# A decoder trunk's embedding gate as seven block products in three passes, with sums of squares kept by accumulating transfers

## The chip, the cores and the metric

The kernel runs on one core of one Trainium2 chip. The metric is device time in microseconds (us), the median over runs. The engines are named as in the profile: PE is the matrix engine (PEld its weight loads), DVE the vector engine, ACT the scalar engine with its activation functions, POOL a general engine that here does elementwise adds and issues transfers, SP an engine that only issues transfers. A matmul multiplies a 128x128 weight block into up to 512 columns (tokens) and adds into a PSUM accumulator. Tiles live on chip with 128 partitions; names that end in `_d` are arrays in device memory (DRAM).

## The reference, cut to what matters

All tensors are float32; 1024 tokens, 2048 features, a per-token embedding `p` of 256.

```python
def rmsnorm(x, g, eps=NORM_EPS):
    y = xf * lax.rsqrt(jnp.mean(xf * xf, axis=-1, keepdims=True) + eps)
    return (y * g.astype(jnp.float32)).astype(x.dtype)
...
        hn = rmsnorm(h, norm_mix_g[i])
        proj = hn @ w_in[i]
...
        mixed = jnp.concatenate([sb_out * jax.nn.silu(sb_g), df_out * jax.nn.silu(df_g)], axis=-1)
        h = h + mixed @ w_out[i]

        gate = jax.nn.sigmoid(rmsnorm(h, norm_ple_g[i]) @ w_ple_gate[i])
        h = h + gate * (p[i] @ w_ple_proj[i])
    return rmsnorm(h, norm_final_g)
```

The change touches the last four of these lines: the out-projection (`w_out`), the gate (`w_ple_gate`, 2048x2048), the embedding's product (`w_ple_proj`, 256x2048) and the two norms around them. The attention before them is untouched.

## The kernel before, in words

Everything is transposed: a tile is 128 features by 512 tokens. The 1024 tokens are two halves of 512; half 1 goes first. 2048 features are 16 tiles, called by `ch` or `kt`.

**Precision.** Each float32 product is made of three matmuls in a faster 32-bit format. An operand x is split into a high part (`xh`, a copy by ACT that rounds) and a low part (`xl` = x - xh, a subtraction by DVE), and so is each weight; the three are xh*whi, xl*whi and xh*wlo. So each weight and each operand costs one ACT and one DVE operation ahead of its first matmul.

**Seven block products.** A product of two 2x2 block matrices takes eight block products; it can be done with seven if sums and differences of blocks are formed first. The class `Seven` (L574) does that for the v and gate projection (`gv`) and the out-projection (`op`, L1350): the operand blocks are half 1 and half 0 of the tokens by two groups of input features, the weight blocks the same groups by the output feature tiles u and u+8. The products are named by the operand they use: A11, A12 and A22 (plain blocks) and S1 to S4 (sums). Weight differences (`T1` to `T4`) are formed by DVE as each product's weights come due; `whigh` and `wlow` split them. `prod` does the twelve matmuls of a product and then splits one further weight and takes up to two entries off the queue `xq` of operand splits. The out-projection runs in two phases `ph`, each over half of the input features, because the operands of one phase fill the chip. In phase 0 the partial results are stored to `half_d`; in phase 1 they are read back (`hr`), added by DVE, and added onto `h_d` (which holds the residual) by an accumulating transfer that POOL issues (`put`, L1365).

**The gate, dense.** The gate comes after the last unit of the out-projection (L1538 on). Its operands are the 16 tiles of h for one half of tokens, times the norm's gain, split by `split` in `gate_loads` (half 1) or `split_scaled` (half 0). `unit(X)` (L218) makes one unit, the output tiles u and u+8 for one half: 4 pieces of 4 input tiles by 2 outputs by 3, 96 matmuls of 512 columns. Weights are loaded and split by `wprep` (L147), 1024 columns at a time, once for each half. First come the eight units of half 1, then the eight of half 0. The norm's root mean square is not needed ahead of the product, because it scales whole tokens: it is multiplied onto the result (`gated`, L1336).

**Around it.** `ple` makes the embedding's product (12 matmuls for each unit and half) into PSUM, and ACT copies it to the chip's memory. `gated` multiplies the gate's result by `rstd`, applies the sigmoid, multiplies by the embedding's product, adds to h, and adds the square of the new h to a sum. These sums of squares (`SumSq`, L101) are ACT squares and POOL adds; a matmul with a matrix of ones adds them over the partitions, and `rstd_from` makes the reciprocal root. `final` scales h and stores the output. The last unit of half 0 (u = 7) is done in two quarters of 256 tokens with weights that are all split ahead (`wz`), so that the first quarter's output is stored while the second is computed.

**Order.** TensorE's order is the order of the program. Up to the third unit of the gate, DVE and ACT also run in the order of the program (`man2`), and after that in an order that a scheduler picks. An engine works through its queue in order: an instruction that waits holds up all that stand behind it. The same holds for SP's and POOL's queues of transfers.

In the out-projection's phase 1 a unit goes A11, A22 of the unit before, S2, S4 of the unit before, A12, S1, S3. In the last unit, A12 (`p2`) stands after S3 instead, ahead of its own A22 and S4.

Of the kernel before, what the change touches and what calls it, by code (L numbers as in the profile page):

```python
# [52 lines left out]
def _body(ctx, nc, tc, ap):  # L53
# [113 lines left out]
    class Stream:  # L167
# [5 lines left out]

        def gates(self):
            units = [ap["w_gate"][u] for _ in range(2) for u in range(8)]
            self.todo = deque((w, pc) for w in units[:-1] for pc in range(4))
            return self.prep(later=True)
# [372 lines left out]
    with tc.tile_pool(name="at", bufs=2) as at, tc.tile_pool(name="pz", bufs=2, space=PSUM) as pz:  # L550
# [23 lines left out]
        class Seven:  # L574

            def __init__(self, w, n):
                self.w = w
                self.units = [(ph, u) for ph in range(2) for u in range(n)]
                self.wq, self.XC, self.T = {}, {}, {}
                self.made, self.late, self.slot = [], 0, 0  # L580
                self.xq = deque()
                self.after = None

            def places(self, nm, i):
                where, t = PLACE[nm][i]
# [7 lines left out]
            def split(self, nm, i, hi, lo, gain=None, raw=None):  # L593

                raw = lo.bitcast(F32) if raw is None else raw
                if gain is None:
                    A.copy(hi, raw)
                    V.tensor_tensor(lo, raw, hi.bitcast(F32), op=ALU.subtract)
                else:
                    A.activation(hi, raw, AF.Copy, scale=gain)  # L600
                    V.scalar_tensor_tensor(lo, raw, gain, hi.bitcast(F32), op0=ALU.mult, op1=ALU.subtract)
                self.XC[nm, i] = hi, lo
# [37 lines left out]
            def begin(self):  # L640
# [3 lines left out]
                self.todo = [e for n in range(len(self.units)) for e in self.sources(n)]  # L644

            def wload(self, n, *bs):
                if n < len(self.units):
# [13 lines left out]
            def sources(self, n):  # L661
# [14 lines left out]
                def t4():  # L676
# [5 lines left out]
                return [(n, nm, fn) for nm, fn in own + [("S2", t2), ("S1", lambda: self.T["T1"]), ("S3", t3),  # L682
                                                         ("S4", lambda: b22_), ("A22", t4)]]

            def whigh(self):
# [3 lines left out]
                n, nm, fn = self.todo[i]  # L689
# [6 lines left out]
                if nm == "S4":  # L696
                    A.activation(t[:, 0], src, AF.Copy, scale=-1.0)
                else:
                    A.copy(t[:, 0], src)  # L699
                self.made.append((src, t))  # L700

            def wlow(self):
# [4 lines left out]
                n, nm, _ = self.todo[i]  # L707
                src, t = self.made[i]
                self.made[i] = None
                if nm == "S4":  # L710
# [3 lines left out]
                ph, u = self.units[n]  # L714
                self.wq[u, ph, nm] = t[:, 0], t[:, 1]
                if nm == "S4":
                    self.wload(n + 2, 22)

            def lead(self):
                for _ in range(4):  # L720
# [4 lines left out]
            def prod(self, u, ph, nm, o, start):  # L725
                self.product(u, ph, nm, o, start)
                self.slot += 1
                self.whigh()
                self.wlow()
                self.after(u, ph, nm)  # L730
                for _ in range(2):
                    if self.xq and self.xq[0][0] <= self.slot:
                        self.xq.popleft()[1]()
# [22 lines left out]
        def split1(c, i):  # L756
            nm = ("A11", "A12")[c]
            gv.split(nm, i, *gv.places(nm, i), gain=gcol(KX[0][i][c]), raw=raw1[i][:, c, :])
# [9 lines left out]
        def combine(i):  # L768
# [4 lines left out]
            def one():  # L773
                gv.split("A22", i, *gv.places("A22", i), gain=gcol(kb), raw=b2)
# [9 lines left out]
        def divide(nm, i):  # L784
            raw = {"S1": raw2[i][1], "S3": raw2[i][0], "S2": raw1[i][:, 0, :], "S4": raw1[i][:, 1, :]}[nm]
            gv.split(nm, i, *gv.places(nm, i), gain=gcol(KX[0][i][0]) if nm == "S3" else None, raw=raw)
# [116 lines left out]
        def load_x(nm, i):  # L903

            hi, lo = gv.places(nm, i)
# [332 lines left out]
        h = {}  # L1238
        hpair = {}
        rst = {}  # L1240
        H1 = (None, None, "k2", "v2", "q", "k", "v", "cs")
        H0 = ("k2", "v2", "q", "bt", "bt", "bt", "pt", "pt")

        def pair(nm, tag, dt=F32, shape=(P, 2, HALF)):
            return at.tile(list(shape), dt, name=nm, tag=tag, bufs=BUFS.get(tag, 2))

        def rows2(nm, u):
            return ap[nm].rearrange("(a k p) t -> k p a t", a=2, p=P)[u]

        def gained(half, ch):  # L1250

            A.activation(h[half, ch], h[half, ch], AF.Copy, scale=gvec[:, 2, ch:ch + 1])

        def final(half, ts, r, us, eng=V):
            o = slice(half * HALF + ts.start, half * HALF + ts.stop)
            for u in us:
                hp = hpair.get((half, u))
                if half == 0 and u == 7:
                    for c in range(2):
                        t = h[half, u + 8 * c][:, ts]  # L1260
                        V.scalar_tensor_tensor(t, t, gvec[:, 2, u + 8 * c:u + 8 * c + 1], r, op0=ALU.mult, op1=ALU.mult)
                elif hp is not None:
                    t = hp[:, :, ts]
                    eng.tensor_tensor(t, t, r.unsqueeze(1).to_broadcast([P, 2, ts.stop - ts.start]), op=ALU.mult)
                else:
                    for c in range(2):
                        t = h[half, u + 8 * c][:, ts]
                        eng.tensor_tensor(t, t, r, op=ALU.mult)
                        nc.sync.dma_start(ap["out"][(u + 8 * c) * P:(u + 8 * c + 1) * P, o], t)
                if hp is not None:  # L1270
                    nc.sync.dma_start(rows2("out", u)[:, :, o], hp[:, :, ts])

        def load_h(half, u):
            tag = (H0, H1)[half][u]
            with tc.issue_after(lastw[0].ins):
# [452 lines left out]
```

## Time and profile before

| | us |
|---|---|
| median of 3 runs | 2491.54 |
| lowest, highest | 2489.08, 2492.83 |
| the profiled execution's own time | 2490.54 |
| its span in the profile | 2488.8 |
| out-projection's last stretch, up to the gate's first matmuls | 2040 to 2063 |
| gate, half 1 | 2063 to 2259 |
| gate, half 0, up to the last unit's quarters | 2273 to 2445 |

The span starts with the first instruction and ends with the last; the execution's own time adds what lies around it. Positions are us from the start of the span. A row of a group view reads: line, engine, operation, output and inputs, shape, count, then total busy time, mean ns of one, and the idle time of the engine just before them with what ended it. A row of single instructions reads: start, duration, engine, line, operation, output and inputs, and in brackets how long the engine stood idle before it and what released it. The granted clock is the share of full speed that the chip allowed TensorE.

### The profile page before, as it was taken

The page shows a single profiled execution, that of the slowest core. Times are in us where ns is not written, and L with a number is a line of the kernel's source. Part 1 is how long each engine was busy: PE and PEld are TensorE (multiplying, and loading weights), DVE is VectorE, ACT ScalarE, POOL GpSimd, SP SyncE. Part 2 cuts the span into 40 slices and gives each one's busy share as a digit, 9 for nine tenths or more (in the row PEclk, how much of TensorE's full clock was granted, in tenths as well). Part 3 has the DMA queues.
Part 4 walks back from the last instruction along what each step waited for, and adds up shares of the span by engine and source line. Part 5 has one row for each costly group of instructions (what it writes and reads, how often), then busy time and mean ns, then how long its engine had stood idle before and what let it go on. Part 6 is the DMA issues. An engine that isn't in the chain of part 4 may idle for free.

```text
span 2488.8 us, 31941 instructions
## 1 busy us (share of the span) xinstructions
PE 2413.1 (97%) x11434; PEld 2002.3 (80%) x11434; DVE 1810.9 (73%) x3010; ACT 1201.2 (48%) x2063; POOL 280.1 (11%) x361
## 2 busy tenths in 40 slices
PE   8999999999999999999999999998899999999997
PEld 6787878888888887888888888886787887787886
DVE  6788777778877778788888877877678674546555
ACT  5334335555555445565555555445423234546342
POOL 1211110000000000000000001110111113330110
PEclk9999999999999999999999999999999999999998
DMA  8776655444445556334444344555757777343433
GB/s 290 250 271 217 224 171 161 154 146 129 145 143 148 181 158 200 119 110 114 121 117 115 102 127 119 144 153 173 224 167 222 165 192 231 121 129 97 133 109 102
DMA packets 167471, 397.72 MB, mean 160 GB/s; under 512 B 18896, under 2 KB 23248, under 8 KB 167312
## 3 DMA queue, kind: packets, MB, share of 16 engines
q1 hardware_dynamic: 131040, 302.07, 37.7%
q0 software_dynamic: 36272, 93.60, 14.3%
q8 instruction: 90, 1.47, 0.2%
q14 instruction: 69, 0.57, 0.1%
HBM read 297.03 MB, written 106.95 MB: 162 GB/s over the span
## 4 chain that ended last, share of the span: by engine, by line
PE 82%; DVE 8%; DMA 4%; ACT 3%; issue 3%; SPq 0%; DVEq 0%; ACTq 0%
PE acc L232 17%; PE acc L233 17%; PE acc L234 17%; PE pbc L611 4%; PE pbc L609 4%; PE pbc L610 4%; PE tp L407 2%; PE z L311 1%; PE z L310 1%; PE pa L611 1%; PE pa L610 1%; PE pa L609 1%; PE av L454 1%; PE av L453 1%; PE av L452 1%
## 5 line engine op out<-in xcount | busy, mean ns | idle before, releaser
L232 PE MATMUL acc<-xh,whi 128*128 128x512 f32 x1568 | 629.0, 401 | 4.0 <-ACT xh L1070 2.5
L234 PE MATMUL acc<-xh,wlo 128*128 128x512 f32 x1568 | 613.8, 391 | 2.2 <-DVE wlo L154 2.2
L233 PE MATMUL acc<-xl,whi 128*128 128x512 f32 x1568 | 613.3, 391 | 0.3 <-DVE xl L1071 0.3
L154 DVE TENSOR_TENSOR wlo<-wraw,whi 128x1024 fp32r<-128x1024 f32 x252 | 312.1, 1239 | 193.3 <-ACT whi L153 187.6
L153 ACT CAST whi<-wraw 128x1024 fp32r<-128x1024 f32 x252 | 264.7, 1050 | 241.3 <-PE acc L233 214.9
L234 PEld LDWEIGHTS acc<-xh,wlo 128*128 128x128 f32 x1568 | 295.0, 188 | 67.5 <-DVE wlo L154 3.5
L232 PEld LDWEIGHTS acc<-xh,whi 128*128 128x128 f32 x1568 | 295.5, 188 | 59.2 <-ACT xh L1070 2.9
L233 PEld LDWEIGHTS acc<-xl,whi 128*128 128x128 f32 x1568 | 296.1, 189 | 54.8 <-DVE xl L1071 0.6
L699 ACT CAST wpr<-T 128x512 fp32r<-128x512 f32 x128 | 78.0, 621 | 317.3 <-DVE T L657 313.0
L426 ACT CAST awh<-tp 128x256 fp32r<-128x256 f32 (+1 forms) x160 | 80.8, 505 | 155.8 <-PE tp L407 155.8
L362 ACT ACTIVATE et<-z,mx 128x512 f32<-128x512 f32 (+7 forms) x128 | 94.8, 741 | 61.1 <-DVE mx L356 52.7
L115 POOL TENSOR_TENSOR ssq<-ssq,sq 128x512 f32<-128x512 f32 x56 | 83.9, 1500 | 304.5 <-ACT sq L114 253.8
L431 DVE TENSOR_TENSOR awl<-tp,awh 128x256 fp32r<-128x256 f32 (+1 forms) x160 | 92.2, 577 | 32.5 <-ACT awh L426 32.4
L356 DVE TENSOR_REDUCE mx<-z 128x1 f32<-128x512 f32 (+7 forms) x128 | 97.0, 758 | 4.4
L341 DVE TENSOR_TENSOR_SCAN st<-pt 128x511 f32<-128x511 f32 (+3 forms) x64 | 86.6, 1353 | 18.0 <-ACT pt L334 16.3
L713 DVE TENSOR_TENSOR wpr<-T,wpr 128x512 fp32r<-128x512 f32 x128 | 87.6, 685 | 6.4 <-ACT wpr L699 4.5
L609 PE MATMUL pbc<-cS,wpr 128*128 128x512 f32 x224 | 87.4, 390 | 3.2 <-DVE u L1485 1.6
L611 PE MATMUL pbc<-cS,wpr 128*128 128x512 f32 x224 | 87.2, 389 | 0.0
L610 PE MATMUL pbc<-cS,wpr 128*128 128x512 f32 x224 | 87.2, 389 | 0.0
L454 PE MATMUL av<-awl,v 128*128 128x256 f32 x256 | 73.8, 288 | 8.4 <-DVE awl L431 8.4
L334 ACT ACTIVATE pt<-z 128x512 f32<-128x512 f32 (+3 forms) x64 | 41.7, 651 | 78.8 <-DVE z L318 73.2
L232 PE MATMUL acc<-cA11h,whi 128*128 128x512 f32 x192 | 76.1, 396 | 0.0
(401 smaller groups left out, 5345.7 us busy)
## 6 DMA issues: line engine op xcount, KB each, us to landing
wraw<-w_in SPq DMA_DIRECT2D x192, 512.0 KB, 3.6
wraw<-w_gate SPq DMA_DIRECT2D x64, 512.0 KB, 3.6
wraw<-w_out SPq DMA_DIRECT2D x72, 256.0 KB, 3.7
wraw<-w_vg SPq DMA_DIRECT2D x71, 256.0 KB, 4.0
comb_d<-sg POOLq DMA_DIRECT2D x48, 256.0 KB, 7.4
spare<-xT SPq DMA_DIRECT2D x44, 256.0 KB, 4.1
xl<-h_d SPq DMA_DIRECT2D x40, 256.0 KB, 5.2
vghalf_d<-hc POOLq DMA_DIRECT2D x32, 256.0 KB, 4.1
```

What stands on the lines that cost most here:

```text
L153: side.later(1, lambda: A.copy(hi[:, o], raw[:, o]))
L154: side.later(side.wlo, lambda: V.tensor_tensor(lo[:, o], raw[:, o], hi[:, o].bitcast(F32), op=ALU.subtract))
L232: T.matmul(acc[c], hi[:, k2, kh, c, :], xh, start=first, stop=False)
L233: T.matmul(acc[c], hi[:, k2, kh, c, :], xl, start=False, stop=False)
L234: T.matmul(acc[c], lo[:, k2, kh, c, :], xh, start=False, stop=last)
L356: V.reduce_max(mx, z[:, vw], axis=AX.X, negate=True)
L362: A.activation(et[:, vw], z[:, vw], AF.Exp, bias=mx[:, 0:1], accum_out=l)
L431: V.tensor_tensor(wl[:, o, :], tp[:, o, :], wh[:, o, :].bitcast(F32), op=ALU.subtract)
L454: T.matmul(av, vv[:, 0, blk % 4, :], wl, start=False, stop=last)
L609: T.matmul(o, wh[:, w], xh, start=start and k == 0, stop=False, skip_group_check=True)
L610: T.matmul(o, wh[:, w], xl, start=False, stop=False, skip_group_check=True)
L611: T.matmul(o, wl[:, w], xh, start=False, stop=k == 3, skip_group_check=True)
```

## The change

The gate becomes a `Seven`-like product too, with all 16 input tiles at once, so that each block product is 8 input tiles by 3, 24 matmuls for an output tile. The operands of all seven don't fit on the chip together, so there are three passes over the eight output units u:

- pass 1: A11 and A12 (`p1`, `p2`), which finish output tile u of half 1; the partial sum after A11 is stored to `part_d`; gating of half 1, tiles 0 to 7 (`gate1`);
- pass 2: S2, S1, S4 (`p6`, `p5`, `p3`), which finish output tile u+8 of half 1; two partial sums go to `q_d`, two weight differences (`second_diffs`) to `tw_d`; gating of half 1, tiles 8 to 15;
- pass 3: S3 and A22 (`begin` and the loop behind it), which finish half 0; the last two units, u = 6 and 7, in two quarters of 256 tokens.

The operands S1 to S4 of the gate are formed during the out-projection's phase 1 (`sums`), whose results stay on the chip (`hq`, `hrows`) for that, and are stored to `hcomb_d`. For that phase 0 now adds its partial results onto `h_d`, and phase 1 reads them back and stores h plainly. The last unit's A12 stands in its normal place. Squares of h are added into four rows of `sq_d` by accumulating transfers (`add_squares`); only the squares of half 1 ahead of the gate and those of half 0 at the end are still added on an engine, DVE. `Seven` gets deferred steps: `soon` holds functions with the slot in which they are due, `split(..., apart)` puts the low part's subtraction a slot later, `lead` prepares six weights ahead where it was four.

```diff
             def lead(self):
-                for _ in range(4):
+                for _ in range(6):
...
+            def step(self):
+
                 self.slot += 1
                 self.whigh()
                 self.wlow()
+                self.due()
+                for _ in range(3 if len(self.xq) > 8 and not self.calm else 2):
+                    e = next((e for e in self.xq if e[0] <= self.slot), None)
...
         def put(o, ph, hf, ch):
 
             if ph:
+                G.dma_start(h_d[hf, ch], o)
+            else:
                 G.dma_start(h_d[hf, ch], o, accum_op=ALU.add)
-            else:
-                G.dma_start(half_d[hf, ch], o)
...
+        def gate_operand(nm, i):
...
+            nc.sync.dma_start(raw, src)
+
+            def fn():
+                if nm in ("A11", "A12"):
+                    if 1 not in ssh:
+                        ssh[1] = ev.tile([P, HALF], F32, name="ssh", tag="rstd1", bufs=1)
+                        A.activation(ssh[1], raw, AF.Square)
+                    else:
+                        for j in range(2):
+                            o = slice(j * 2 * P, j * 2 * P + 2 * P)
+                            s = ev.tile([P, 2 * P], F32, name="s", tag="sm", bufs=5)
+                            A.activation(s, raw[:, o], AF.Square)
+                            op.soon.append((op.slot + 1, partial(V.tensor_tensor, ssh[1][:, o], ssh[1][:, o], s, op=ALU.add)))
+                op.split("g" + nm, i, hi, lo, gain, apart=True)
...
+        def second_diffs(u, ks):
+            b11, b12, b21, b22 = [raws[u % 2, ks, b] for b in (11, 12, 21, 22)]
+            V.tensor_tensor(b11, b12, b11, op=ALU.subtract)
+            t2 = at.tile([P, 4 * P], F32, name="T2", tag="awl")
+            V.tensor_tensor(t2, b22, b11, op=ALU.subtract)
+            V.tensor_tensor(b12, b12, b22, op=ALU.subtract)
+            V.tensor_tensor(b21, b21, t2, op=ALU.subtract)
...
+        def sums(u, hq, a2, b1):
...
+            def one():
+                A.activation(b2, b2, AF.Copy, scale=gb)
+                V.scalar_tensor_tensor(b2, a2, ga, b2, op0=ALU.mult, op1=ALU.add)
+                store("S1", b2)
+                V.tensor_tensor(a2, a2, a1, op=ALU.subtract)
+                store("S3", a2)
+
+            def two():
+                V.scalar_tensor_tensor(a1, a1, ma, b2, op0=ALU.mult, op1=ALU.add)
+                store("S2", a1)
+                V.scalar_tensor_tensor(b1, b1, mb, a1, op0=ALU.mult, op1=ALU.add)
+                store("S4", b1)
...
-                if last:
-                    gate0 = stream.gates()
-                    p2()
...
+        def gprod(u, nm, o, start):
+            for ks in range(2):
+                wh, wl = op.wq.pop((u, "g" + nm, ks))
+                for k in range(4):
+                    xh, xl = op.XC["g" + nm, 4 * ks + k]
+                    w = slice(k * P, k * P + P)
+                    T.matmul(o, wh[:, w], xh, start=start and ks + k == 0, stop=False, skip_group_check=True)
+                    T.matmul(o, wh[:, w], xl, start=False, stop=False, skip_group_check=True)
+                    T.matmul(o, wl[:, w], xh, start=False, stop=ks == 1 and k == 3, skip_group_check=True)
...
+                op.step()
...
+        def add_squares(half, s):
+
+            n = nsq[half]
+            nsq[half] += 1
+            G.dma_start(sq_d[half, n % 2], s, **(dict(accum_op=ALU.add) if n > 1 else {}))
...
+            def gate():
+                V.tensor_tensor(o, o, z, op=ALU.mult)
+                V.tensor_tensor(hc[u + 8 * c], hc[u + 8 * c], o, op=ALU.add)
+
+            def squared():
+                t = hc.pop(u + 8 * c)
+                A.activation(o, t, AF.Square)
+                A.dma_start(h_d[1, u + 8 * c], t)
+                add_squares(1, o)
...
+        def p1(u):
...
+            gprod(u, "A11", pa[u], True)
+            s1 = ev.tile([P, HALF], F32, name="s1", tag="sq", bufs=2)
+            A.copy(s1, pa[u])
+            A.dma_start(part_d[u], s1)
+
+        def p2(u):
+            gprod(u, "A12", pa[u], False)
...
+        def squares0(n):
...
+                t = ev.tile([P, HALF], F32, name="hs", tag=("rstd0", "ssq")[n % 2], bufs=1)
+                nc.sync.dma_start(t, h_d[0, ch])
...
+        def p6(u):
...
+            gprod(u, "S2", b, True)
+            V.tensor_tensor(w, b, w, op=ALU.add)
+            G.dma_start(q_d[u, 0], w)
...
+        def begin(u):
+
+            bs[u] = pp.tile([P, HALF], F32, name="pb", tag="acc", bufs=2)
+            gprod(u, "S3", bs[u], True)
...
+            def embedded():
+                ple(0, u, 1, z)
+                ple(0, u, 0, zs[u])
...
+        for tq in range(2):
...
+            for u in (6, 7):
...
+                partly(u, "S3", b[u], ts, True)
...
+            for u in (6, 7):
+                partly(u, "A22", b[u], ts, False)
```

More of the change, by code (lines that the diff above doesn't have):

```diff
@@ L773, in one @@
             def one():
-                gv.split("A22", i, *gv.places("A22", i), gain=gcol(kb), raw=b2)
+                gv.split("A22", i, *gv.places(PLACE["A22"][i], "A22"), gain=gcol(kb), raw=b2)
             def two():
@@ new lines, in _body @@
+        p2(1)
+        norm([ssh[1]])
+        embedding(1)
+        plew_load(0, 0)
+        plew_load(1, 0)
+        p1(3)
+        load_hc(0)
+        load_hc(1)
+        plew(0, 0)
+        squares0(0)
+        p2(2)
+        gate1(0)
+        squares0(1)
+        p1(4)
+        gate1(1)
+        squares0(2)
+        p2(3)
+        gate1(2)
+        squares0(3)
+        p1(5)
+        gate1(3)
+        squares0(4)
+        p2(4)
+        gate1(4)
+        squares0(5)
+        p1(6)
+        squares0(6)
@@ L1651, in _body @@
[L1651 to L1662 removed]
+            b = {}
```

735 lines of the change are left out of this document (449 added, 286 removed).

## The prediction

> **What bounds the kernel now.** I read the page's busy shares first, then the chain of work that ended last, then busy time by stretch, then TensorE's single instructions where the stretches show a hole.
>
> ```profile
> span 2488.8 us, 31941 instructions
> PE 2413.1 (97%) x11434; PEld 2002.3 (80%) x11434; DVE 1810.9 (73%) x3010; ACT 1201.2 (48%) x2063; POOL 280.1 (11%) x361
> ...
> PE 82%; DVE 8%; DMA 4%; ACT 3%; issue 3%; SPq 0%; DVEq 0%; ACTq 0%
> ```
>
> TensorE is busy 97% and holds 82% of the chain. A share over the whole span doesn't price a change in one stage, so here are the stages (columns: stretch, its length, busy us of PE, PEld, DVE, ACT and POOL, granted clock, DMA share, GB/s):
>
> ```profile
> 10.00:30.00 20.00, 17.35 (x55) 12.69 (x55) 9.47 (x14) 10.97 (x17) 2.18 (x4) 0.86 1.05 389
> 1926.00:2040.00 114.00, 114.00 (x504) 93.94 (x503) 77.05 (x120) 27.01 (x48) 20.41 (x24) 1.00 0.74 168
> 2040.00:2063.00 23.00, 20.42 (x89) 16.27 (x88) 21.19 (x33) 12.32 (x21) 4.25 (x5) 1.00 0.99 265
> 2063.00:2259.00 196.00, 194.49 (x857) 160.41 (x856) 94.64 (x106) 103.80 (x145) 64.62 (x44) 1.00 0.47 150
> 2259.00:2273.00 14.00, 9.50 (x27) 5.94 (x25) 9.53 (x15) 11.16 (x16) 0.00 (x0) 0.78 0.41 128
> 2273.00:2445.00 172.00, 172.00 (x753) 141.38 (x752) 86.41 (x90) 69.20 (x88) 17.37 (x11) 1.00 0.35 112
> ```
>
> The gate runs from 2063 to the end. In its two long stretches TensorE is full (194.5 of 196, 172 of 172) at full clock, DVE and ACT are at about half, the DMA engines at 0.35 to 0.47. So a matmul taken out of the gate saves its whole time, as long as the other engines keep up. The end of the out-projection (2040 to 2063) differs: DVE 21.2 of 23 us, DMA 0.99, TensorE has holes.
>
> What one matmul costs must be read from the starts, since neighbours overlap:
>
> ```profile
> 2425.38 0.39 PE L234 MATMUL acc<-xh,wlo 128*128 128x512 f32 x1
> 2425.61 0.39 PE L232 MATMUL acc<-xh,whi 128*128 128x512 f32 x1
> 2425.83 0.39 PE L233 MATMUL acc<-xl,whi 128*128 128x512 f32 x1
> 2426.06 0.39 PE L234 MATMUL acc<-xh,wlo 128*128 128x512 f32 x1
> ```
>
> Each row shows 0.39 us, but three starts span 0.68 us: a 512-wide matmul costs 0.2267 us, and 0.39 would overstate the gain by 70%.
>
> **The change, part by part.** (1) *Matmuls.* A dense 2x2 block product is eight block products, the new one seven. Each gate unit has 16x2x3 = 96 matmuls per half, 192 for both; seven eighths are 168. Eight units lose 24 each: 192 fewer 512-wide matmuls (the last units are cut into quarters before and after alike). Embedding products stay. 192 x 0.2267 = **-43.5 us**. Both ends are the same: only a wait can eat it.
>
> (2) *The change of halves.* The dense gate finishes half 1, then splits half 0's operands and embedding:
>
> ```profile
> 2261.17 0.39 PE L1331 MATMUL ple<-ph,pwl 128*128 128x512 f32 x1
> 2264.41 0.49 PE L1329 MATMUL ple<-ph,pwh 128*128 128x512 f32 x1 [2.85 <-ACT ph L1301]
> ...
> 2267.78 0.80 PE L1330 MATMUL ple<-pl,pwh 128*128 128x512 f32 x1 [0.92 <-DVE pl L1302]
> ...
> 2269.22 0.63 PE L1330 MATMUL ple<-pl,pwh 128*128 128x512 f32 x1
> 2269.65 0.63 PE L1331 MATMUL ple<-ph,pwl 128*128 128x512 f32 x1
> ...
> 2271.36 1.91 PE L127 MATMUL ssps<-ssq,onesr 128*128 128x512 f32 x2
> ...
> 2273.49 0.48 PE L233 MATMUL acc<-xl,whi 128*128 128x512 f32 x1
> ```
>
> The 12.3 us from 2261.17 to 2273.49 hold 13 matmuls worth 2.9 us and the sum of squares (1.9): 7.5 us are lost to the wait for the embedding's split and to the 0.43 us pitch of the slowed clock behind it. After, half 0's embedding is split ahead of S3 of unit 0, whose 24 matmuls (5.4 us) cover it. **-7.5**, ends -7.5 and 0 (if the split is late again).
>
> (3) *Stalls that go with the old code*, the norm's wait and the two of the last out-projection unit: **-1.5** and **-2.6**.
>
> ```profile
> 2056.26 0.47 PE L609 MATMUL pbc<-cA,wpr 128*128 128x512 f32 x1 [1.80 <-DVE hc L1515]
> 2060.01 0.50 PE L609 MATMUL pbc<-cS4h,wpr 128*128 128x512 f32 x1 [0.79 <-DVE hc L1456]
> 2138.91 0.47 PE L232 MATMUL acc<-xh,whi 128*128 128x512 f32 x1 [1.51 <-DVE gt L1341]
> ```
>
> (4) *DVE, ACT and POOL.* Durations by shape:
>
> ```profile
> L154 DVE TENSOR_TENSOR wlo<-wraw,whi 128x1024 fp32r<-128x1024 f32 x60 | 78.1, 1302 | 144.7 <-ACT whi L153 140.5 <-PE ssps L127 4.2
> L1434 DVE SCALAR_TENSOR_TENSOR xl<-xl,gvec,xh 128x512 fp32r<-128x512 f32 x16 | 11.2, 747 | 2.3 <-ACT xh L1433 2.3
> L1515 DVE TENSOR_TENSOR hc<-pbc,u 128x512 f32<-128x512 f32 x7 | 4.8, 691 | 0.2
> L1659 DVE TENSOR_TENSOR h<-h,gt 128x256 f32<-128x256 f32 x4 | 1.7, 423 | 0.1
> L1433 ACT ACTIVATE xh<-xl,gvec 128x512 fp32r<-128x512 f32 x16 | 10.5, 713 | 0.0
> L115 POOL TENSOR_TENSOR ssq<-ssq,sq 128x512 f32<-128x512 f32 x56 | 83.9, 1500 | 304.5 <-ACT sq L114 253.8 <-ACT ssq L110 48.6
> ```
>
> Weight splits go from 64 of 1024 columns to 112 of 512; 64 weight differences, 24 more operand splits and 32 sums (four per out-projection unit) are new. In out-projection phase 1 DVE has 24 operations of 0.69 = 16.5 us per unit under 84 matmuls = 19.0. In the gate, pass 1 has 54 matmuls = 12.25 us per unit with some 5 us of DVE, pass 2 78 = 17.7 us with some 20 operations = 14, pass 3 60 = 13.6 us with at most 12. All stay under TensorE: 0 on the path, but at 80 to 87% of a unit a late operand is caught up slowly. For such waits in the passes **+3**, ends 0 and +15 (22 units, 0.7 each, as the second stall in 3). POOL's 56 adds go; its 1.5 us each lay beside full stretches, so 0.
>
> (5) *The walk from out-projection to gate.* This is the part that speaks against the change. Before, A12 of the last unit stood between S3 and A22 as filler; now A22(7) follows S3(7) at once and needs DVE's three adds (3 x 0.69 = 2.1) that read both halves of its PSUM tile; the stall on L1515 in (3) shows that a product into one half waits for the read of the other. Ahead of these adds in DVE's queue stand two gate operands with their squares, 2 x (0.42 + 0.42 + 0.75) = 3.2. Their h rows are loaded only when A12(7) frees the place:
>
> ```profile
> xl<-h_d SPq DMA_DIRECT2D x40, 256.0 KB, 5.2
> h_d<-hc POOLq DMA_DIRECT2D x30, 256.0 KB, 5.2
> wraw<-w_gate SPq DMA_DIRECT2D x64, 512.0 KB, 3.6
> ...
> q1 hardware_dynamic: 6101, 11.13, 41.6%
> q0 software_dynamic: 2885, 5.25, 30.4%
> ```
>
> So 5.2 landing, 1.55 on ACT (two halves of squares at 0.42, one 0.71), 3.2 and 2.1 on DVE, less S1 and S3 (5.4): 6.6 us, at least 2.5. S4(7) waits for A22's read behind two lows: 2.5, ends 0.8 and 3. The second half of A12's first gate product needs operands 4 to 7, loaded after S4(7) and split between sums and weight lows: 5, ends 0 and 7.5. A gap of 6.6 us would also slow the clock, as the 3.0 us gap in (2) did: 2. In all **+16**, ends +4 and +20.
>
> [...]
>
> (6) *The tail*: both end with two token quarters, square sums and eight stores: 0, up to +1 for two more short gating chains.
>
> Sum: 2490.5 (the profiled execution's own time) - 43.5 - 7.5 - 1.5 - 2.6 + 16 + 3 = 2454.4. The median shown lies 1.0 above the profiled one: **2455 us**; its own range, with all ends, 2441 to 2480.
>
> **The rivals.** *A, pass 1 is bound by transfers.* By the diff pass 1 moves some 30 MB plain (8 of its weights; operands, h rows, stores, the next pass's weights) and 5 MB accumulating. The fastest stretch moved 389 GB/s (10 to 30); in 1940 to 2040 the accumulating queue, q0 above, took 30.4 us of all engines for 5.25 MB, 173 GB/s. That is 78 + 29 = 107 us against 98 of matmuls, 9 too many; and SP's loads of h rows wait for a place that an accumulating store (5.2) holds, ahead of weights with a lead of some 2.72 us per half product: 8 units x 2.4 = 19 at worst. Between: 2455 + 20 = **2475**. Against: part is prefetch for pass 2.
>
> *B, slower: the accumulating DMAs line up.* The 32 stores into four rows of sums read, add and write the same bytes; if POOL's queue waits for each to land, everything behind waits too: pass 1 has 19 of them. At 5.2 they take 99 us against 98: even. Loaded, a store on that queue took 7.4 (the gate sums' row):
>
> ```profile
> comb_d<-sg POOLq DMA_DIRECT2D x48, 256.0 KB, 7.4
> ```
>
> Then pass 1 needs 141 us, 43 too many, and pass 2 (13 of these and 16 plain at 3.3 or more) 149 against 141: 2455 + 51 = **2506**. It decides from about 7 us each. For it: tiles that the gating needs again are held by these stores. Against: the rows alternate, so only every second one meets its predecessor, and 83.9 us of POOL's adds (L115) leave at the same time.
> [...] No row here shows two on one row.
>
> *C, the walk is free* because the loads land early: only the lower ends, **2442**. *D, the change doesn't do what it says*: seven products but the path elsewhere, on DVE say, **2490**; DVE was busy 94.6 of 196 us, so little speaks for it.
>
> **How the numbers follow.** Forecast 0.58, A 0.16, C 0.12, B 0.11, D 0.03. 2440 to 2484 takes in the forecast's ends, C, and A's most, and leaves out B and D. About 0.2% is what a measurement here can tell from none (5 us). Faster 0.58 + 0.12 + 0.15 = 0.85; within 0.2% 0.04; slower 0.11.
>
> **What would show it.** Right: 192 fewer 512-wide matmuls at a pitch of 0.227 in the passes; no hole like 2261 to 2273; a hole of 5 to 8 us ahead of the last A22 on DVE. Wrong: DMA share near 1 and weights as releasers in pass 1 (A), POOL busy with waits between square sums (B), or no hole at the walk (C).

## The result, and the profile after

| | before | after |
|---|---|---|
| median of 5 runs, us | 2491.54 (2488.42 to 2492.83) | 2483.09 (2478.19 to 2483.33) |
| ratio to before, 95% interval | | 0.9964 (0.9950 to 0.9979) |
| profiled execution, own time | 2490.54 | 2478.19 |
| its span | 2488.8 | 2476.4 |

The change is faster by 8 us, where 36 were forecast. The profiled execution of the changed kernel is the fastest of its five. A further profile of it (the control below) has a span of 2479.7, with holes at the same places; there the first hole of the crossing is split into two, of 2.2 and 2.6 us.

The page of the changed kernel, busy time and chain:

```profile
span 2476.4 us, 32496 instructions
...
PE 2374.1 (96%) x11250; PEld 1967.5 (79%) x11250; DVE 1905.4 (77%) x3288; ACT 1199.1 (48%) x2151; POOL 231.0 (9%) x353
...
PE 78%; DMA 8%; DVE 7%; ACT 3%; issue 3%; SPq 0%; POOL 0%; ACTq 0%; DVEq 0%; POOLq 0%
```

TensorE has 184 matmuls fewer (192 dense ones fewer, eight more for the norm of the last quarters), and its share of the chain fell from 82 to 78%, while transfers rose from 4 to 8%. Busy time by stretch (columns: stretch, its length, busy us of PE, PEld, DVE, ACT and POOL, granted clock, DMA share, GB/s):

```profile
2063.00:2080.00 17.00, 12.53 (x47) 9.61 (x46) 13.54 (x27) 9.88 (x24) 1.62 (x3) 0.90 1.04 393
2160.00:2180.00 20.00, 19.85 (x88) 16.12 (x87) 9.90 (x16) 5.41 (x11) 2.03 (x4) 1.00 0.98 290
2180.00:2200.00 20.00, 16.00 (x64) 12.65 (x63) 10.53 (x18) 8.14 (x16) 3.07 (x4) 0.91 1.07 358
2200.00:2220.00 20.00, 14.77 (x56) 11.12 (x55) 18.34 (x31) 9.16 (x17) 4.59 (x7) 0.91 1.03 306
2220.00:2240.00 20.00, 20.00 (x90) 16.57 (x89) 15.73 (x27) 7.58 (x14) 3.53 (x5) 1.00 1.04 356
```

From 2220 on TensorE is full at the old pitch (90 matmuls in 20 us). The loss stands where one stage meets the next. The matmuls that end TensorE's holes, from its single instructions:

```profile
1806.29 0.77 PE L614 MATMUL pbc<-cS,wpr 128*128 128x512 f32 x1 [12.64 <-DVE u L1590]
...
2067.49 0.74 PE L614 MATMUL pbc<-cA,wpr 128*128 128x512 f32 x1 [3.68 <-DVE hq L1616]
...
2072.86 0.50 PE L614 MATMUL pbc<-cS4h,wpr 128*128 128x512 f32 x1 [0.78 <-DVE hc L1517]
...
2096.45 0.80 PE L1640 MATMUL pa<-cgA12l,wpr 128*128 128x512 f32 x1 [3.81 <-DVE cgA12l L601]
...
2185.91 0.50 PE L1562 MATMUL z<-ph,pwhl 128*128 128x512 f32 x1 [4.00 <-ACT pwhl L1554]
...
2204.01 0.79 PE L1641 MATMUL pb<-cgS,wpr 128*128 128x512 f32 x1 [3.48 <-DVE wpr L724]
...
2455.41 0.28 PE L1967 MATMUL pbq<-cgA22h,wpr 128*128 128x256 f32 x1
2460.05 1.22 PE L2004 MATMUL ssps<-sq,onesr 128*128 128x256 f32 x2 [4.37 <-ACT sq L2001]
```

To price them with the slowed clock behind them, I summed, place by place, how far the starts of neighbouring matmuls lie apart beyond 0.2267 us for each 512 columns:

| place (us in the trace after) | lost before | lost after | difference |
|---|---|---|---|
| end of the attention (1763 to 1782) | 1.3 | 3.6 | +2.3 |
| start of the out-projection's S products (1791 to 1811) | 6.5 | 15.3 | +8.9 |
| within the out-projection (1912 to 1933) | 3.3 | 1.8 | -1.4 |
| walk to the gate (2063 to 2102) | 3.1 | 14.7 | +11.6 |
| pass 1 to pass 2 (2111 to 2213) | 0 | 14.3 | +14.3 |
| norms and change of halves | 12.0 | 1.7 | -10.2 |
| first quarters (2441 to 2448) | 0.4 | 1.2 | +0.8 |
| last product to the end | 17.25 | 20.99 | +3.7 |
| matmuls, 192 x 0.2267 | | | -43.5 |

The sum is -13.5; the spans differ by -12.4.

### The profile page after: what moved, and what is told of

It is laid out like the page before. It is cut to its first block, busy times and chain, and to the rows that moved or that the text cites. A ratio compares the mean times of both kernels' runs of the same rounds, so it can differ in the third digit from the quotient of the medians.

```text
span 2476.4 us, 32496 instructions
## 1 busy us (share of the span) xinstructions
PE 2374.1 (96%) x11250; PEld 1967.5 (79%) x11250; DVE 1905.4 (77%) x3288; ACT 1199.1 (48%) x2151; POOL 231.0 (9%) x353
## 4 chain that ended last, share of the span: by engine, by line
PE 78%; DMA 8%; DVE 7%; ACT 3%; issue 3%; SPq 0%; POOL 0%; ACTq 0%; DVEq 0%; POOLq 0%
PE acc L227 13%; PE acc L229 13%; PE acc L228 13%; PE pbc L614 4%; PE pbc L616 4%; PE pbc L615 4%; PE tp L402 2%; PE z L306 1%; PE z L305 1%; PE pa L615 1%; PE pa L616 1%; PE pa L614 1%; PE av L449 1%; PE av L448 1%; PE pb L1639 1%
## 5 line engine op out<-in xcount | busy, mean ns | idle before, releaser
L227 PE MATMUL acc<-xh,whi 128*128 128x512 f32 x1152 | 465.2, 404 | 2.5 <-ACT xh L1104 2.5
L229 PE MATMUL acc<-xh,wlo 128*128 128x512 f32 x1152 | 451.3, 392 | 2.2 <-DVE wlo L154 2.2
L228 PE MATMUL acc<-xl,whi 128*128 128x512 f32 x1152 | 450.6, 391 | 0.3 <-DVE xl L1105 0.3
L154 DVE TENSOR_TENSOR wlo<-wraw,whi 128x1024 fp32r<-128x1024 f32 x192 | 234.2, 1220 | 48.5 <-ACT whi L153 47.1
L153 ACT CAST whi<-wraw 128x1024 fp32r<-128x1024 f32 x192 | 201.7, 1051 | 120.7 <-PE acc L228 112.0
L229 PEld LDWEIGHTS acc<-xh,wlo 128*128 128x128 f32 x1152 | 216.4, 188 | 51.1 <-DVE wlo L154 3.5
L227 PEld LDWEIGHTS acc<-xh,whi 128*128 128x128 f32 x1152 | 217.0, 188 | 40.6 <-ACT xh L1104 2.9
L228 PEld LDWEIGHTS acc<-xl,whi 128*128 128x128 f32 x1152 | 217.4, 189 | 37.9 <-DVE xl L1105 0.6
L710 ACT CAST wpr<-wraw 128x512 fp32r<-128x512 f32 x112 | 68.6, 614 | 105.6 <-DMA wraw<-tw_d 36.3
L614 PE MATMUL pbc<-cS,wpr 128*128 128x512 f32 x224 | 88.4, 395 | 14.3 <-DVE u L1590 12.6
L724 DVE TENSOR_TENSOR wpr<-wraw,wpr 128x512 fp32r<-128x512 f32 x112 | 75.6, 685 | 21.9 <-ACT wpr L710 21.8
```

The source lines that it names most:

```text
L153: side.later(1, lambda: A.copy(hi[:, o], raw[:, o]))
L154: side.later(side.wlo, lambda: V.tensor_tensor(lo[:, o], raw[:, o], hi[:, o].bitcast(F32), op=ALU.subtract))
L227: T.matmul(acc[c], hi[:, k2, kh, c, :], xh, start=first, stop=False)
L228: T.matmul(acc[c], hi[:, k2, kh, c, :], xl, start=False, stop=False)
L229: T.matmul(acc[c], lo[:, k2, kh, c, :], xh, start=False, stop=last)
L614: T.matmul(o, wh[:, w], xh, start=start and k == 0, stop=False, skip_group_check=True)
```

## The experiments

Every run stands beside runs of the kernel before on its chip. All ratios are to that kernel, with 95% intervals. Lost times are from each run's trace, one execution each, worked out as in the table. The kernel before took 2488.9 to 2491.5 us on the chips used, so runs on different chips are best compared by their ratios.

### The lead of six weights

The hole at 1793 is in a part that the prediction didn't price. DVE in the changed kernel at that time:

```profile
1791.91 0.68 DVE L722 SCALAR_TENSOR_TENSOR wpr<-wraw,wpr 128x512 fp32r<-128x512 f32 x1
1801.11 0.69 DVE L669 TENSOR_TENSOR T<-wraw 128x512 f32<-128x512 f32 x1 [8.51 <-issue]
1801.83 0.69 DVE L669 TENSOR_TENSOR T<-b,T 128x512 f32<-128x512 f32 x1
1802.44 1.46 DVE L724 TENSOR_TENSOR wpr<-T,wpr 128x512 fp32r<-128x512 f32 x2
1804.25 1.29 DVE L599 TENSOR_TENSOR cA<-cA 128x512 fp32r<-128x512 f32 x2 [0.35 <-ACT cA L593]
1805.46 0.68 DVE L1590 TENSOR_TENSOR u<-pbc,s 128x512 f32<-128x512 f32 x1
```

In the kernel before, `u` stood ahead of that `T`:

```profile
1792.30 0.69 DVE L1485 TENSOR_TENSOR u<-pbc,s 128x512 f32<-128x512 f32 x1
1798.09 0.69 DVE L657 TENSOR_TENSOR T<-wraw 128x512 f32<-128x512 f32 x1 [5.11 <-issue]
```

TensorE waits for the sum `u`. In the changed kernel it stands in DVE's queue behind `T`, a weight difference of the *next* unit. The profile names no releaser for `T` ("issue"); its inputs are blocks whose loads SP could issue only as the first unit's differences were made (from 1785 to 1812 SP waited 11.9 us for them). So the suspects are the fifth and sixth weight of the lead.

```diff
             def lead(self):
-                for _ in range(6):
+                for _ in range(4):
```

> The changed kernel with four weights prepared ahead at the start of the out-projection instead of six (and so four ahead through all passes of the gate). Theory lead: the hole of 12.6 us on TensorE at 1793 in the changed kernel's trace comes from the fifth and sixth weight, whose differences need blocks of the next unit; DVE stands in front of a load that has not landed, with the operands' splits behind it. Expected: the hole shrinks to the 4 to 5 us (1.60, 1.38, 1.12 and a slower clock) of the kernel before, 9 to 12 us faster than the changed kernel (about 2472), minus what a lead of four loses in the gate (0 to 5). Rival: the loads are late by themselves, the hole stays within 3 us of 12.6 and the time within 3 us of 2483.

Measured: 2501.0 us, ratio 1.0054 (1.0037 to 1.0071). The time is a miss: some 2472, or up to 5 more, was expected. The hole fell as expected, from 15.3 to 9.0 us lost, but a lead of four starves pass 2: each unit loses 1.1 us at S2, the crossing of passes 25 and its end 7.5 instead of nothing. So the gate needs the six; the out-projection pays for them.

The kernel before, with `range(6)` in the same line:

> The kernel before with six weights prepared ahead instead of four, nothing else. Theory lead: the hole at 1793 appears here too, 12 to 13 us instead of 1.6, and the time is 9 to 12 us over the kernel before (ratio about 1.004). Rival: it needs something else of the change, ratio 1.000.

Measured: 2499.17 us, ratio 1.0045 (1.0030 to 1.0060), 10.2 us over the kernel before on that chip. Its hole:

```profile
1803.57 0.76 PE L609 MATMUL pbc<-cS,wpr 128*128 128x512 f32 x1 [11.76 <-DVE u L1485]
```

One number in the old kernel makes the whole hole: the theory is shown. Of the 10.2 us its trace shows 7.5 at this place (14.1 lost for 6.6) and 3.5 more at 1910 to 1936, where the changed kernel loses less than the kernel before; so the price for the change is the table's 8.9, not 10.2. The changed kernel with the two weights later:

```diff
-                for _ in range(6):
+                for _ in range(4):
...
                 self.slot += 1
-                self.whigh()
-                self.wlow()
+                for _ in range(2 if self.slot in (8, 10) else 1):
+                    self.whigh()
+                    self.wlow()
```

> The changed kernel with four weights prepared at the start of the out-projection and the fifth and sixth two and four products later, so that the gate still finds six. Theory lead: the hole at 1793 (12.6 us, 15 with the slowed clock) shrinks to the 4 to 9 us that the run with four throughout showed, and pass 2 keeps its weights: 6 to 11 us faster than the changed kernel, ratio to the kernel before about 0.993. Rival: the two later weights make the same hole a few products later; ratio 0.996.

Measured: 2474.33 us, ratio 0.9937 (0.9922 to 0.9951), some 7 us faster than the change, as expected; 7.9 us are lost at this place instead of 15.3. TensorE's holes there:

```profile
1796.96 0.47 PE L614 MATMUL pbc<-cS,wpr 128*128 128x512 f32 x1 [1.59 <-DVE u L1591]
1805.45 0.50 PE L614 MATMUL pbc<-cS2h,wpr 128*128 128x512 f32 x1 [2.77 <-ACT wpr L710]
1807.30 0.56 PE L616 MATMUL pbc<-cS2h,wpr 128*128 128x512 f32 x1 [1.12 <-DVE wpr L724]
```

These are the kernel before's own three waits at this place, the middle one longer:

```profile
1793.13 0.47 PE L609 MATMUL pbc<-cS,wpr 128*128 128x512 f32 x1 [1.60 <-DVE u L1485]
1800.21 0.50 PE L609 MATMUL pbc<-cS2h,wpr 128*128 128x512 f32 x1 [1.38 <-ACT wpr L699]
1802.06 0.50 PE L611 MATMUL pbc<-cS2h,wpr 128*128 128x512 f32 x1 [1.12 <-DVE wpr L713]
```

### The crossing from pass 1 to pass 2

Two holes, 4.0 us at 2181 and 3.5 at 2200, cost 14 us with the slowed clock and the smaller waits behind them. The transfers issued from 2160 to 2210 (output and input, issuing engine, count, size of one, median us from issue to landing), and ACT's instructions that stood waiting there (start, duration, engine, line, operation; in brackets the idle time and its releaser):

```profile
wraw<-w_gate SPq DMA_DIRECT2D x19, 256.0 KB, 5.7
...
cgS4l<-hcomb_d SPq DMA_DIRECT2D x8, 256.0 KB, 6.3
...
s<-part_d SPq DMA_DIRECT2D x2, 256.0 KB, 7.4
```

```profile
2194.40 1.31 ACT L593 CAST cgS4h<-cgS4l 128x512 fp32r<-128x512 f32 x2 [6.45 <-DMA cgS4l<-hcomb_d]
2195.62 0.40 ACT L1554 CAST pwhl<-pw 128x256 fp32r<-128x256 f32 x1
...
2204.30 0.63 ACT L1736 ACTIVATE hs<-hs 128x512 f32<-128x512 f32 x1 [5.30 <-DMA hs<-h_d]
```

Transfers are slow (a gate weight took 3.6 us before, with twice the bytes), and ACT stands in front of them with weights queued behind. Two causes are possible: the burst, or the order of ACT's queue. Without most squares of half 0 (14 of 16 tiles are left out):

```diff
         def squares0(n):
 
+            if n > 1:
+                return
```

> The changed kernel without the squares of half 0 for 14 of 16 tiles (their loads of h and their accumulating transfers are left out, so half 0's first norm is of two tiles only). Theory transfers: the waits of 4.0, 3.5 and 1.0 us at 2181 to 2213 (some 13 us with the slowed clock) come from DMA engines that are full there (share 1.0 from 2140 on), so 14 times 256 KB loaded and 256 KB accumulated fewer bring operands and weights in time: 8 to 13 us faster. Rival queue order: the operands S2, S1 and S4 are late because their places come free late and SP's queue is in order, whatever else is moved: under 3 us faster.

Measured: 2475.71 us, ratio 0.9951 (0.9937 to 0.9966). In the trace the first hole is gone and the second keeps 5.7 us: 6.6 lost at the crossing for 14.3, so about half of the loss goes. The time shows less. By the ratios the run is 3 us below the change, at the edge of what the rival gave, and the intervals overlap. Its profiled execution was 8 us behind the change's by the end of the attention, which this edit doesn't touch.

All transfers of squares as plain writes (28 sums are left out):

```diff
-            G.dma_start(sq_d[half, n % 2], s, **(dict(accum_op=ALU.add) if n > 1 else {}))
+            G.dma_start(sq_d[half, n % 2], s, **{})
```

> The changed kernel with all transfers of squares to the rows of sums as plain writes instead of accumulating ones (28 sums are left out: each row holds the last square). If the read, add and write of an accumulating transfer is the price, the same number of transfers without it brings most of the 8 to 13 us of the run without squares of half 0; if only bytes and places count, under 4 us. If they had been waiting on each other (the slower rival of the prediction), more than 10 us.

Measured: 2478.35 us, ratio 0.9962 (0.9947 to 0.9977), no different from the change (0.9964). The crossing lost 12.1. Here the accumulation costs nothing that can be measured. Whether the transfers line up is read from the change's own trace: its 32 transfers of squares took 6.8 us to land (median), but it shows no wait of one for another. Where POOL stood idle ahead of one, ACT's square ended the wait (25 times, 209 us in all), and TensorE lost nothing from 2113 to 2176, most of pass 1. So rival B falls.

S4's splits three products later:

```diff
-            e = [(op.slot + 2, gate_operand(nm, i0 + j)) for j in range(4)]
+            e = [(op.slot + (5 if nm == "S4" else 2), gate_operand(nm, i0 + j)) for j in range(4)]
```

> The changed kernel with the splits of S4's eight operands queued three products later (their loads stay where they are). Theory queue: at 2188 to 2194 ACT stands 6.45 us in front of an operand of S4 that has not landed, and the next unit's embedding weights and S2 weights wait behind it; later splits free ACT, so the hole of 3.5 us at 2200 and those after it (7.7 us in all) go to under 3: about 5 us faster, ratio 0.994. Rival transfers: the weights themselves land late, the hole stays, ratio 0.996.

Measured: 2484.26 us, ratio 0.9975 (0.9963 to 0.9987): no gain, and the crossing lost 19.8. ACT stood 12.4 us in front of a load of h for the squares instead, and then S4's own operand was late (1.85 us at 2220):

```profile
2207.08 0.63 ACT L1736 ACTIVATE hs<-hs 128x512 f32<-128x512 f32 x1 [12.41 <-DMA hs<-h_d]
```

So order alone, in this form, only hands the wait on. The three squares that fall on the crossing moved into pass 2, nothing left out, beside a control:

```diff
         second_places()
-        squares0(8)
...
         gate1(6)
-        squares0(9)
...
         gate1(7)
-        squares0(10)
...
-            if 11 + u < 16:
-                squares0(11 + u)
+            if u < 5:
+                squares0(8 + max(0, 2 * u - 1))
...
+            if 1 <= u < 4:
+                squares0(8 + 2 * u)
```

> The changed kernel again, beside the three that follow on one chip: ratio to the kernel before 0.995 to 0.998, with the hole of 12 to 13 us at 1793 and the holes at 2181 and 2200 in the same places.

Measured: 2481.27 us, ratio 0.9970 (0.9960 to 0.9979).

> The changed kernel with the three squares of half 0 that fall on the crossing from pass 1 to pass 2 (tiles 8 to 10: load of h, square, accumulating transfer) moved into pass 2, nothing left out. Theory: their loads are late in SP's queue and in full DMA engines, and ACT waits in front of them (5.3 us at 2204), so without them the crossing's holes (13.9 us in all) shrink by 5 to 7 us as without any squares of half 0: about 2477 and ratio 0.994. Rival: the operands and weights are late whatever else is there; under 2 us.

Measured: 2480.57 us, ratio 0.9962 (0.9950 to 0.9974): a miss, within the rival's 2 us. The crossing lost 12.9, the control 15.2. With the later weights of the lead:

> Moved squares together with the later fifth and sixth weight: the two losses lie 370 us apart, so the gains add, 11 to 14 us faster than the changed kernel, ratio about 0.991. If the crossing was only a matter of being early or late against the transfers, the lead's gain alone, 0.9935.

Measured: 2470.63 us, ratio 0.9925 (0.9913 to 0.9937), 10.6 below the control, just short of the sum; the crossing lost 11.0.

Then the order again, milder, with the squares out of the way: S4 and the second half of S1 two products later.

```diff
-            e = [(op.slot + 2, gate_operand(nm, i0 + j)) for j in range(4)]
+            e = [(op.slot + (4 if nm == "S4" or (nm, i0) == ("S1", 4) else 2), gate_operand(nm, i0 + j)) for j in range(4)]
```

> Moved squares and later fifth and sixth weight, and the splits of S4 and of S1's second four operands queued two products later than there. Theory order: at 2177 to 2194 ACT stands in front of these operands' loads while the embedding's weights and S2's weights wait behind, so the two holes of the crossing (10 to 11 us with the slowed clock) go to under 4: 6 us faster than without this edit (2470.6). Rival burst: 13 MB have to land in the 40 us ahead of 2200, so what is asked for last is late in any order: within 2 us.

Measured: 2468.96 us, ratio 0.9916 (0.9901 to 0.9931): below the run before by 1.7 us in the medians and 2 by the ratios, with intervals that overlap. That is about what the rival gave, and a miss for the order. The first hole fell from 3.3 to 0.7, the second grew; the crossing lost 8.7 for 11.0. And both at once, order as here and 14 tiles' squares left out:

> As the run before, with the squares of half 0 left out for 14 of 16 tiles (their loads and accumulating transfers), so that the burst is some 2 MB smaller and pass 2 lighter. If order and burst share the loss, the crossing is under 2 us here and the time 4 us below the run before; if order is all, equal to it; if burst is all, 5 us below with holes as in the run without squares.

Measured: 2458.84 us, ratio 0.9876 (0.9861 to 0.9890), 10.1 us below the run before, where 4 or 5 were expected; 2.3 us of the difference between the two traces are there by the attention's end, which the edit doesn't touch. The stretches of this run:

```profile
2160.00:2180.00 20.00, 20.00 (x90) 16.57 (x89) 14.36 (x25) 8.40 (x16) 1.71 (x2) 1.00 1.03 349
2180.00:2200.00 20.00, 18.96 (x84) 15.38 (x83) 17.34 (x29) 8.77 (x16) 2.55 (x4) 1.00 1.06 361
2200.00:2220.00 20.00, 20.00 (x90) 16.54 (x89) 18.11 (x31) 7.81 (x15) 2.01 (x3) 1.00 0.98 324
```

The crossing loses 1.7 us. That the squares are about half of the loss is shown twice: without them the crossing lost 7.7 us less in the change (14.3 to 6.6) and 7.0 less with the order and the lead of this run (8.7 to 1.7). The order's part is less sure. With the moved squares it took 2.3 us off in the trace (11.0 to 8.7), which the times can't tell from nothing; without them 4.9 (6.6 to 1.7), but there the later weights of the lead came with it. So no single edit takes the loss away, and the order's share is argued in part.

Nor do these runs show what it is about the squares that costs: with them go bytes, places in SP's queue, and ACT's waits for their loads. The DMA engines are as full here as in the change (1.03 and 1.06), and a gate weight takes as long to land (6.0 us for 5.7).

### The tail

```diff
             if tq:
-                final(slice(0, Q), r2)
+                final(slice(0, Q), r2, range(2))
+                with tc.issue_after(lsq.ins):
+                    final(slice(0, Q), r2, range(2, 8))
```

Here `lsq` is the second quarter's last square. In the change, DVE does the first quarter's scalings just when the last products end (their last matmul starts at 2455.41):

```profile
2452.94 3.70 DVE L1879 TENSOR_TENSOR h<-h,r 128x512 f32<-128x512 f32 x6
2456.55 1.67 DVE L1876 SCALAR_TENSOR_TENSOR h<-h,gvec,r 128x256 f32<-128x256 f32 x4
...
2458.46 0.76 DVE L1989 TENSOR_TENSOR qt<-pbq,qt 128x256 f32<-128x256 f32 x2
```

In the kernel before, most of them were done when the last product's last matmul started, at 2471.55. The last row of each of the two views is the first step of the last product's gating, 1.7 us behind that matmul here and 3.1 in the change:

```profile
2467.59 3.09 DVE L1264 TENSOR_TENSOR h<-h,r 128x512 f32<-128x512 f32 x5
...
2470.94 1.28 DVE L1264 TENSOR_TENSOR h<-h,r 128x512 f32<-128x512 f32 x2
...
2473.27 0.42 DVE L1656 TENSOR_TENSOR gt<-acq,rstd 128x256 f32<-128x256 f32 x1
```

> The changed kernel with six of the eight output scalings of the first token quarter held back until the second quarter's last square. Theory tail: after the last product DVE is 5.3 us in the first quarter's scalings (2452.9 to 2458.2) before it starts on the second quarter's gating, so the norm is late; held back, they fill DVE's wait for the norm instead: 2 to 3 us less from the last product to the end (21.0 us in the changed kernel, 17.1 before). Rival: ACT's table loads and the longer chain of four gated tiles set it; under 1 us.

Measured: 2479.96 us, ratio 0.9963 (0.9950 to 0.9975). In the trace the stretch from the last product to the end falls from 21.0 to 18.9 us, as expected, and it is 18.9 in the three other runs with this edit too; in the medians 2 us is within the spread. The remaining 1.6 us over the kernel before (17.25) stay open; the expectation's rival, ACT's table loads and a chain of four gated tiles, was not tried.

### Sums

Later weights of the lead, S4's splits three products later and later scalings together:

> The three edits together (later fifth and sixth weight, later splits of S4, later scalings). If the three losses are separate their gains add: 13 to 19 us faster than the changed kernel, ratio to the kernel before about 0.990. If the pass 1 to 2 crossing only moves its wait, about 0.992.

Measured: 2474.27 us, ratio 0.9934 (0.9919 to 0.9949): a miss, the lead's gain and no more, since the crossing lost 18.1 with S4's later splits.

The same three and the moved squares:

> Moved squares, later fifth and sixth weight, later splits of S4 and later scalings together. With the squares gone from the crossing the later splits of S4 free ACT for the weights: hole at 2200 under 3 us, tail 2 us shorter, ratio about 0.989, the fastest of all. If S4 is late then instead, not better than without that edit (0.991).

Measured: 2472.29 us, ratio 0.9930 (0.9915 to 0.9945): a miss again. S4 three products later costs more than the tail wins (crossing 15.0, for 11.0 without it).

The moved squares, the later weights and the later scalings, with S4 where the change has it:

> Moved squares, later fifth and sixth weight and later scalings, splits of S4 where the change has them: the sum of the three without the edit that brought nothing. 2 us faster than without the scalings (2470.6), so about 2468.5, ratio 0.9915; not under 2470 if the tail's gain is lost in the spread.

Measured: 2466.76 us, ratio 0.9907 (0.9891 to 0.9924), as expected, and the fastest kernel that computes everything: 24 us below the kernel before on its chip, 14.5 to 16.3 below the change's two medians. How much of the 3.9 us to 2470.63 is the tail's isn't settled: the two were timed on different chips, and the trace gives the tail 2.1.

## Why the prediction was wrong in size

The sign was right. The median of 2483 lies above the forecast's own range (2441 to 2480) and just inside the wider one, which had room for rival A up to 2484. The forecast of 36 us was 28 too much by the medians, 24 by the profiled executions. The steps that failed are the lead of six, the waits in the passes and the tail.

- *Matmuls, -43.5*: right. The pitch in pass 2 is the old one, and the trace has the fewer matmuls.
- *Change of halves and norm, -7.5 and -1.5*: right, -10.2 together. What is left are the norm's matmuls.
- *Walk, +16*: right in sum, 14.7, and for the reasons given, but in part by luck, since its parts were off: A22(7) waited 3.7 instead of 6.6, S4(7) 0.8 instead of 2.5, A12's operands 4.8 as forecast (5), and the slowed clock took the rest, 5.4 instead of 2, since it slowed twice. The gap in part 2 that the clock's 2 us lean on is 2.85 us by its row, not 3.0.
- *The lead of six, not priced*: this is the step that failed first. Part 4 counted DVE's and ACT's work per unit and concluded "All stay under TensorE: 0 on the path"; it didn't ask where two more weights stand in DVE's queue at the start. They cost 8.9 us in the trace, and put alone into the kernel before they make the same hole.
- *Waits in the passes, "+3, ends 0 and +15"*: mis-sized, and the largest miss. The +3 had no working of its own, and the end of +15 stood for 22 waits of 0.7 us on late operands. What the trace has is one place, the crossing, with 14.3; that this fits under the end of 15 is luck. The rest of the three passes lost under 2. This is close to rival A's mechanism, transfers and queues, though not all along pass 1 as A had it (DMA share 0.68 to 0.76 from 2080 to 2140) but where operands, weights of the next pass and squares are all asked for at once. How the loss divides between transfers and the order of the queues stays open in part.
- *Tail, "0, up to +1 for two more short gating chains"*: mis-sized, +3.7. The chains are short; what I missed is that the first quarter's 5.4 us of scalings now stand in front of the last product's gating, which starts 3.1 us behind its last matmul, for 1.7 before. Held back, they give 2.1 of the 3.7 back; 1.6 stay open.
- *B* fell: that the transfers of squares wait for one another was assumed, the change's trace shows no such wait, and plain writes bring nothing. *C* and *D* fell too: the walk has its hole, though of 3.7 us ahead of A22 and not the 5 to 8 that were to show it, and the gate has its gain.

The three misses are 8.9 + 11.3 + 3.7 = 23.9. The attention's end, which the change doesn't touch, and the first quarters took 3.1 more; walk, out-projection and the change of halves did 4.4 better than the forecast. That makes 22.6 of the 24, and the rest is what the table's sum leaves. Why the attention's end loses more stays open. It was later in every trace of a changed kernel: the attention's last matmul started at 1782.5 to 1790.7 us in these 15, and at 1780.3 and 1780.6 in the kernel before and in the one with `range(6)`.

## What to carry to other kernels

A per-unit balance of engine time tells whether a stage can run, not how it starts: price each change of how far ahead work is prepared by walking the in-order queue to the first instruction that needs data not yet loaded, and by listing what stands behind it. Where one pass hands over to the next, count the transfers asked for in that window and move out those that can wait, then look at what stands in the queue behind a late load. Here the first won about half in the traces, delaying the consumers of late loads won nothing or little alone, and both together won nearly all. A lead is cheap in steady state and dear at the start, so grow it after the start.

## What the runs showed of the hardware that I had not expected

The clock can slow after a hole is over. Behind 3.33 us of idle time (the run of later weights and moved squares) the pitch (from start to start) was near its normal 0.23 us for five matmuls, and then 0.43:

```profile
2180.53 0.50 PE L1563 MATMUL z<-ph,pwhl 128*128 128x512 f32 x1 [3.33 <-ACT pwhl L1555]
2180.86 0.40 PE L1564 MATMUL z<-pl,pwhl 128*128 128x512 f32 x1
...
2181.57 0.41 PE L1564 MATMUL z<-pl,pwhl 128*128 128x512 f32 x1
2181.80 0.60 PE L1565 MATMUL z<-ph,pwhl 128*128 128x512 f32 x1
2182.20 0.63 PE L1640 MATMUL pb<-cgS,wpr 128*128 128x512 f32 x1
2182.63 0.63 PE L1641 MATMUL pb<-cgS,wpr 128*128 128x512 f32 x1
```

So a hole of 3.3 us cost 5.2 in all. In the record of the granted clock of the kernel before and of the changed one, each stretch at half clock (0.50) up to the tail lasts 3.41 us or a whole multiple of it (6.83, and the 13.65 that begin inside the changed kernel's hole of 12.64); where TensorE is full in it, one of 3.41 us costs 1.7, half its length (an estimate from these two numbers). The clock also halved behind shorter holes. In the run of later scalings the pitch doubled five matmuls behind a hole of 1.76 us:

```profile
2178.17 0.50 PE L1639 MATMUL paz<-cgA12h,wpr 128*128 128x512 f32 x1 [1.76 <-ACT s L1713]
...
2179.44 0.59 PE L1641 MATMUL paz<-cgA12h,wpr 128*128 128x512 f32 x1
2179.82 0.63 PE L1639 MATMUL paz<-cgA12h,wpr 128*128 128x512 f32 x1
2180.25 0.63 PE L1640 MATMUL paz<-cgA12l,wpr 128*128 128x512 f32 x1
```

Nor does the length of a hole alone tell it. In the kernel before, a stretch at half clock began at 1717.3, just behind a hole of 1.85 us, and none behind one of 2.02, where the granted clock from 1701 to 1711 is 1.00:

```profile
1701.05 0.55 PE L407 MATMUL tp<-ident,bt 128*128 128x128 f32 x3 [2.02 <-DVE sm L463]
...
1716.69 0.39 PE L454 MATMUL av<-awl,v 128*128 128x256 f32 x1 [1.85 <-DVE awl L431]
```

The runs show no threshold for the idle time.

Loads also took longer where the DMA engines were full: in the change a 256 KB gate weight took 5.7 us from issue to landing where the share was 1.0 (2160 to 2210), in the kernel before a 512 KB one 3.6 where it was 0.4 (2070 to 2440).
